# Norm chains between layers and at the end cut into halves, their squares moved forward, and one split of the last down projection made early

## The chip, the cores and the metric

The kernel runs on one core of a Trainium2 chip, in float32 throughout. The metric is the device time of one execution in microseconds; the times shown are medians of several runs. TensorE's clock has two levels here, 1.2 and 2.4 GHz; the profile gives what was granted as a share of the upper one.

## The reference

Two transformer blocks stand one behind the other, for 512 tokens of width 1024 (batch 1). What matters here is how they begin and end:

```python
def _rmsnorm(x, g):
    y = x * rsqrt(mean(x * x, axis=-1) + 1e-6)
    return y * g

# first block
h  = _rmsnorm(x, g_pre_mix)
...                                            # retention, spatial gating, merged
x  = x + _rmsnorm(merged @ w_out, g_post_mix)  # 1024 x 1024
h2 = _rmsnorm(x, g_pre_ffn)
x  = x + _rmsnorm(mlp(h2) @ w_down, g_post_ffn)  # 2816 x 1024, mlp starts with h2 @ w_up
# second block
h  = _rmsnorm(x, attn_norm_w)
...                                            # two kinds of attention, mixed
x  = x + mix @ w_out                           # 1024 x 1024, no norm behind it
h2 = _rmsnorm(x, mlp_norm_w)
u  = relu(h2 @ w_up)                           # 1024 x 4096
x  = x + (u * u) @ w_down                      # 4096 x 1024
return _rmsnorm(x, final_norm_w)
```

## The kernel before

**Products.** Each float32 operand of a large product is split into a high and a low part of the matmul's reduced float32 (`split`, line 145: ScalarE copies the high part, VectorE subtracts to get the low part), and a product is three matmuls: high high, high low, low high (lines 243 to 247). Weights come in units of 128 x 1024 values (512 KB) through three raw buffers; each is split as well, first part on ScalarE (line 220), second part on VectorE or, for some, on GpSimd (line 208). `W.advance` emits the second parts of units whose first parts are there and then further first parts, up to three units ahead of the one in use.

**Two kinds of stages.** `dense_a` gives features on the partitions and all 512 tokens as columns, 24 matmuls of 512 columns for a group of 128 features; with `first=4` the first four groups are done for tokens 0 to 255 before tokens 256 to 511. `dense_bs` gives tokens on the partitions; at the second block's start it takes token tiles (0, 1) ahead of (2, 3), in 12 matmuls of 256 columns per weight unit and tile. `down` (line 341) gives tokens on the partitions and 1024 columns in eight PSUM banks, two halves c = 0, 1 for each of four token tiles t. It runs over K outermost, but the last four K tiles go by token: for each (t, c) twelve matmuls, then a tick, then `finish(t, c)`. So the tiles' results come one after the other, each half 2.7 us apart.

**The order of work.** All instructions are emitted in the order in which the program is written, and each engine takes its own in that order. Side work is written as generators (class `Weave`): a task yields how long it waits, in units of a group of 24 matmuls, and `tick(w)` counts this down for all tasks; one whose count reaches zero emits its next piece at that point. `tick` of the kernel first calls `W.advance`. A tick is thus no time but a place in the queues.

**The chains between layers.** Behind `w_out` and `w_down` of the first block, `finish` runs `post_chain`: `post_norm` (line 485) takes the Square of the first PSUM half with its sum over the row (ScalarE), and when the second half is done the Square of that; GpSimd adds the two sums (line 492), scales and adds EPS (line 440) and takes the power -1/2 (line 441); VectorE multiplies each half by it and by g (`y`, line 497); the sum x + y is done by GpSimd for the first half and by VectorE for the second (line 499). After a wait of 0.5 follows `norm_T` (line 450) for the next layer: Square of the whole row of 1024 (line 447), the two GpSimd operations, after 0.5 `xn` in one VectorE instruction (line 454), after 0.5 eight transposes on TensorE (line 460) into two PSUM banks and the split of each bank (lines 147, 148). `dense_a` and `dense_bs` finish the chains of the tiles that they need first. Behind `w_out_2` there is no norm ahead of the sum: `finish` adds PSUM to x (line 1209) and starts `norm_T`. At the start `norm_T` takes the tiles of x as they land.

**The last down projection.** Its left operand, the 32 feature tiles of `u2`, is split in pairs by `lazy` (line 827): `pair(kp)` makes pair kp, where it isn't there, and kp + 1, in a buffer of the pool `big`. The first call, at the stage's beginning, makes pairs 0 and 1. `finish` (line 1234) adds PSUM to x, takes the Square of the half, and after the second half GpSimd forms the factor; VectorE multiplies both halves by it and by g (line 1250), and each half goes out by a DMA of its own (256 KB), the first issued by SyncE, the second by ScalarE (line 1251).

Of the kernel before, what the change touches and what calls it, by code (L numbers as in the profile page):

```python
# [8 lines left out]
F32R = mybir.dt.float32r  # L9
# [51 lines left out]
class Weave:  # L61
    """Side work emitted between groups of dense matmuls. A task yields how long to wait, in units
    of a group of 24 matmuls of 512 columns."""
# [44 lines left out]
def tile_kernel(  # L108
# [36 lines left out]
    def split(hi, lo, src, eng=None):  # L145
        """src = hi + lo exactly, both rounded to the matmul's reduced float32."""
# [40 lines left out]
    class Stream:  # L187
# [24 lines left out]
        def advance(self, lead):  # L212
            """second parts of the units whose first parts are there, then the next first parts"""
# [29 lines left out]
    def mm(q, lhs, rhs, start, stop):  # L243
        """float32 product of split operands: hi hi + hi lo + lo hi."""
# [4 lines left out]
    class Act:  # L249
        """split activations, features on partitions: [P, K, T] as halves of four tiles of K."""  # L250
# [12 lines left out]
    def dense_a(units, act, evac, first=0, K=KD, pend=None):  # L263
        """features x tokens; of the first so many features, half of the tokens before the rest."""
# [45 lines left out]
    def dense_bs(chunks, act, groups, pend=None):  # L310
        """tokens x columns, K outermost; all chunks for one group of token tiles after the other"""
# [29 lines left out]
    def down(src, K, act_pair, finish):  # L341
        """tokens x 1024 columns: K outermost but for the last four tiles, which go by tokens."""
# [36 lines left out]
    def gload(name, eng=None):  # L379
        """g on every partition."""  # L380
# [53 lines left out]
    def rpow(src, scale, name):  # L434
        """1 / sqrt(scale src + EPS)"""
        r = sm(1, name)
        if scale == 1.0:
            nc.gpsimd.tensor_scalar(r, src, EPS, None, op0=ALU.add)
        else:
            nc.gpsimd.tensor_scalar(r, src, scale, EPS, op0=ALU.mult, op1=ALU.add)  # L440
# [3 lines left out]
    def rms(xt):  # L444
        """1 / rms of the rows"""
        ss = sm(1, "ss")
        nc.scalar.activation(junk, xt, AF.Square, accum_out=ss)
# [851 lines left out]
```

## Time and profile before

| | |
|---|---|
| three runs | 1616.9 us median (1616.67 to 1617.52) |
| span of the profiled execution | 1614.6 us (its own time isn't given apart; the median of the runs is 2.3 us longer than this span) |
| granted TensorE clock, mean | 0.993 |
| TensorE busy | 1577.2 us, 7832 matmuls |
| VectorE, ScalarE, GpSimd busy | 762.3, 614.3, 330.6 us |

The page's other parts show that the transfers take a third of the DMA engines' time or less after the start. A row of a timeline gives start, duration, engine, source line, operation, the tile written and those read with their shapes, the number of instructions merged (x2), and in brackets how long the engine was idle before and for what it waited. PE is TensorE, DVE VectorE, ACT ScalarE, POOL GpSimd; a q behind the name is its queue of DMA issues.

### The profile page before, as it was taken

Reading aid. Unit: us, or ns where it says so; the run is one execution under the profiler, and the core shown is the slowest. Engines: PE = TensorE matmul, PEld = TensorE weight load, DVE = VectorE, ACT = ScalarE, POOL = GpSimd, SP = SyncE. Lnnn points to the kernel's source line nnn. Section 1 sums busy time; section 2 is a strip of 40 time slices with the busy share of each in tenths; the row PEclk is TensorE's granted clock in tenths of the full one; section 3 lists DMA queues with packets and bytes.
Section 4 is the critical chain, followed back from the end, with each engine's and each line's share of the span. In section 5 each row is a group of like instructions: output and inputs, shape, how many; then the busy total and the mean of one; then the engine's idle time right before and its main releaser. Section 6 shows DMA issues by size and latency. Waiting matters only on the chain.

```text
span 1614.6 us, 19745 instructions
## 1 busy us (share of the span) xinstructions
PE 1577.2 (98%) x7832; PEld 1320.6 (82%) x7832; DVE 762.3 (47%) x1305; ACT 614.3 (38%) x1012; POOL 330.6 (20%) x301
## 2 busy tenths in 40 slices
PE   8999999999999999999999999999999999999998
PEld 7888888888887888888887887777877988878886
DVE  4247322453546454555335788768443322233333
ACT  4233223322324433333334366675833322233322
POOL 1015000241004111211004443333244210010000
PEclk9999999999999999999999999999999999999999
DMA  7322332213442233334321412222133333332221
GB/s 210 104 92 65 92 118 85 73 53 91 127 147 65 79 92 102 94 92 136 117 95 56 144 53 53 79 59 74 65 126 95 92 104 97 86 118 96 100 92 52
DMA packets 187323, 152.27 MB, mean 94 GB/s; under 512 B 5232, under 2 KB 157424, under 8 KB 186720
## 3 DMA queue, kind: packets, MB, share of 16 engines
q1 hardware_dynamic: 184784, 143.65, 29.4%
q0 software_dynamic: 1584, 5.70, 1.0%
q10 hardware_dynamic: 864, 1.67, 0.3%
q8 instruction: 61, 1.00, 0.3%
q14 instruction: 30, 0.25, 0.1%
HBM read 146.81 MB, written 4.19 MB: 94 GB/s over the span
## 4 chain that ended last, share of the span: by engine, by line
PE 83%; DVE 8%; ACT 3%; POOL 2%; issue 2%; DMA 1%; SPq 0%; DVEq 0%; POOLq 0%; ACTq 0%
PE ps L245 26%; PE ps L246 26%; PE ps L247 25%; DMA wr<-in_w_in_dram 1%; PE ps L973 1%; PE ps L1064 1%; DVE work L990 1%; PE ps L1055 1%; PE ps L466 1%; PE ps L733 1%; POOL Ya L1188 1%; ACT pr L1034 1%; ACT wh L220 1%; POOL rstd L441 1%; DVE xs L499 1%
## 5 line engine op out<-in xcount | busy, mean ns | idle before, releaser
L220 ACT ACTIVATE wh<-wr 128x1024 fp32r<-128x1024 f32 (+1 forms) x259 | 271.0, 1051 | 250.0 <-PE ps L247 130.9
L208 DVE TENSOR_TENSOR wl<-wr,wh 128x1024 fp32r<-128x1024 f32 (+1 forms) x212 | 257.8, 1226 | 178.9 <-ACT wh L220 178.8
L245 PE MATMUL ps<-wh,ls 128*128 128x512 f32 x432 | 168.4, 390 | 1.2 <-ACT ls L147 1.2
L247 PE MATMUL ps<-wh,ls 128*128 128x512 f32 x432 | 168.2, 389 | 0.3 <-DVE ls L148 0.3
L246 PE MATMUL ps<-wl,ls 128*128 128x512 f32 x432 | 168.1, 389 | 0.0
L246 PE MATMUL ps<-h2Tl,wh 128*128 128x512 f32 (+1 forms) x384 | 142.7, 372 | 0.3 <-DVE h2Tl L148 0.3
L245 PE MATMUL ps<-h2Th,wh 128*128 128x512 f32 (+1 forms) x384 | 142.8, 372 | 0.0
L247 PE MATMUL ps<-h2Th,wl 128*128 128x512 f32 (+1 forms) x384 | 142.6, 371 | 0.0
L208 POOL TENSOR_TENSOR wl<-wr,wh 128x1024 fp32r<-128x1024 f32 x47 | 114.8, 2449 | 134.6 <-ACT wh L220 134.4
L245 PE MATMUL ps<-hTh,wh 128*128 128x512 f32 (+1 forms) x288 | 107.3, 373 | 0.2 <-ACT hTh L147 0.2
L246 PE MATMUL ps<-hTl,wh 128*128 128x512 f32 (+1 forms) x288 | 105.7, 367 | 0.5 <-DVE hTl L148 0.3
L247 PE MATMUL ps<-hTh,wl 128*128 128x512 f32 (+1 forms) x288 | 105.5, 366 | 0.0
L245 PE MATMUL ps<-h3Th,wh 128*128 128x512 f32 (+1 forms) x288 | 105.4, 366 | 0.0
L246 PE MATMUL ps<-h3Tl,wh 128*128 128x512 f32 (+1 forms) x288 | 105.3, 365 | 0.0
L247 PE MATMUL ps<-h3Th,wl 128*128 128x512 f32 (+1 forms) x288 | 105.2, 365 | 0.0
L245 PEld LDWEIGHTS ps<-wh,ls 128*128 128x128 f32 x432 | 81.1, 188 | 18.4 <-ACT ls L147 1.6
L247 PEld LDWEIGHTS ps<-wh,ls 128*128 128x128 f32 x432 | 81.1, 188 | 17.7 <-DVE ls L148 0.8
L246 PEld LDWEIGHTS ps<-wl,ls 128*128 128x128 f32 x432 | 81.1, 188 | 16.6
L857 ACT ACTIVATE hid<-ps,cols 128x512 f32<-128x512 f32 x44 | 34.3, 781 | 144.8 <-PE ps L247 144.8
L858 DVE SCALAR_TENSOR_TENSOR hid<-ps,cols,hid 128x511 f32<-128x511 f32 x44 | 33.0, 749 | 116.8 <-ACT hid L857 116.8
L865 POOL TENSOR_TENSOR act<-hid 128x512 f32<-128x512 f32 x22 | 45.2, 2055 | 194.1 <-DVE hid L860 180.1
L246 PEld LDWEIGHTS ps<-h2Tl,wh 128*128 128x128 f32 x384 | 72.3, 188 | 13.0 <-DVE h2Tl L148 0.6
(293 smaller groups left out, 3253.7 us busy)
## 6 DMA issues: line engine op xcount, KB each, us to landing
wr<-in_w_in_dram SPq DMA_DIRECT2D x86, 512.0 KB, 3.7
wr<-in_w_up_dram SPq DMA_DIRECT2D x76, 512.0 KB, 4.0
wr<-in_w_down_dram SPq DMA_DIRECT2D x54, 512.0 KB, 3.6
wr<-in_w_out_dram SPq DMA_DIRECT2D x16, 512.0 KB, 3.6
wr<-in_w_sgu_o_dram SPq DMA_DIRECT2D x8, 512.0 KB, 4.1
wr<-in_w_ret_o_dram SPq DMA_DIRECT2D x8, 512.0 KB, 4.0
g<-in_rows_dram POOLq DMA_DIRECT2D x6, 512.0 KB, 6.9
x<-in_x_dram SPq DMA_DIRECT2D x4, 512.0 KB, 8.3
```

What stands on the lines that cost most here:

```text
L208: eng.tensor_tensor(lo, self.raw.pop(i), hi.bitcast(F32), ALU.subtract)
L220: nc.scalar.activation(hi, self.raw[self.n_hi], AF.Copy)
L245: nc.tensor.matmul(q, lhs[0], rhs[0], start=start, stop=False)
L246: nc.tensor.matmul(q, lhs[0], rhs[1], start=False, stop=False)
L247: nc.tensor.matmul(q, lhs[1], rhs[0], start=False, stop=stop)
L441: nc.gpsimd.tensor_tensor(r, r, nhalf, ALU.pow)
L466: nc.tensor.transpose(q[:, i * P:(i + 1) * P], src[:, i * P:(i + 1) * P], ident)
L499: eng.tensor_tensor(xrow(t)[:, sl], xrow(t)[:, sl], y[:, sl], ALU.add)
L733: nc.tensor.matmul(o, kz[:, d, c - d, :], vc[c], start=True, stop=True)
L857: nc.scalar.activation(o, q, AF.Identity, bias=col("conv_b", f), scale=col("conv_w1", f))
L858: nc.vector.scalar_tensor_tensor(o[:, 1:], q[:, :T - 1], col("conv_w0", f), o[:, 1:], ALU.mult, ALU.add)
L865: nc.gpsimd.tensor_tensor(act[fa // 4][:, fa % 4, :], a, b, ALU.mult)
```

## The change

The mean is taken inside the Square: ScalarE scales by 1/sqrt(1024) before it squares, so that the accumulated sum is the mean's share of a half, and one GpSimd instruction adds the two halves and EPS (`rpow2`). Every Square and `xn` goes by halves of 512. In `post_norm` both sums x + y are VectorE's, and the Square of each x half is emitted right behind it; its results are handed on to `norm_T`, which then begins with the factor. `norm_T` by itself emits its Squares first and the factor a quarter of a group later; before, the factor's operations were emitted together with the Square. `down` ticks twice for each (t, c), 0.25 in the middle of the twelve matmuls and 0.25 at the end. Pair 0 of the last down projection is split behind the Relu of feature tile 28, in two buffers of the temporary pool `tp`. In the last `finish` the tile t = 3 gets its first half multiplied by g when c = 0 is done, and ScalarE scales this by the factor while VectorE does the second half; the first half now goes out by ScalarE's queue, the second by SyncE's.

```diff
-                tick(0.5)
+                    if kp == n - 2:          # inside the loop over the tail's K pairs
+                        tick(0.25)
...
+                tick(0.25)
                 wv.cur = 0
                 finish(t, c, q2[t])
...
+    def rpow2(ss, name):
+        r = sm(1, name)
+        nc.gpsimd.tensor_scalar(r, ss[:, 1:2], ss[:, 0:1], EPS, op0=ALU.add, op1=ALU.add)
+        nc.gpsimd.tensor_tensor(r, r, nhalf, ALU.pow)
+        return r
+
+    def square(src, acc):
+        w = src.shape[-1]
+        nc.scalar.activation(junk[:, :w], src, AF.Square, scale=D ** -0.5, accum_out=acc)
...
-    def norm_T(t, xt, g, dst, lag=0.5):
-        r = rms(xt)
-        yield lag
+    def norm_T(t, xt, g, dst, lag=0.5, ss=None):
+        if ss is None:
+            ss = sm(2, "ss")
+            for c in range(2):
+                square(xt[:, c * 512:(c + 1) * 512], ss[:, c:c + 1])
+            yield 0.25
+        r = rpow2(ss, "rstd")
         xn = tmp([P, D], "xn")
-        nc.vector.scalar_tensor_tensor(xn, xt, r, g, ALU.mult, ALU.mult)
+        for c in range(2):
+            sl = slice(c * 512, (c + 1) * 512)
+            nc.vector.scalar_tensor_tensor(xn[:, sl], xt[:, sl], r, g[:, sl], ALU.mult, ALU.mult)
         yield lag
...
     def post_norm(t, q, g):
         ss = sm(2, "ss2")
-        nc.scalar.activation(junk[:, :512], q[0], AF.Square, accum_out=ss[:, 0:1])
+        square(q[0], ss[:, 0:1])
         yield 99
-        nc.scalar.activation(junk[:, :512], q[1], AF.Square, accum_out=ss[:, 1:2])
-        s1 = sm(1, "ss1")
-        nc.gpsimd.tensor_tensor(s1, ss[:, 0:1], ss[:, 1:2], ALU.add)
-        r = rpow(s1, 1.0 / D, "rstd2")
+        square(q[1], ss[:, 1:2])
+        r = rpow2(ss, "rstd2")
         y = tmp([P, D], "y")
+        sx = sm(2, "ss")
         for c in range(2):
             sl = slice(c * 512, (c + 1) * 512)
             nc.vector.scalar_tensor_tensor(y[:, sl], q[c], r, g[:, sl], ALU.mult, ALU.mult)
-            eng = (nc.gpsimd, nc.vector)[c]
-            eng.tensor_tensor(xrow(t)[:, sl], xrow(t)[:, sl], y[:, sl], ALU.add)
-        yield 0.5
+            nc.vector.tensor_tensor(xrow(t)[:, sl], xrow(t)[:, sl], y[:, sl], ALU.add)
+            square(xrow(t)[:, sl], sx[:, c:c + 1])
+        yield 0.75
+        return sx
...
-                yield from post_norm(t, q, g)
-                yield from norm_T(t, xrow(t), g_next, dst)
+                sx = yield from post_norm(t, q, g)
+                yield from norm_T(t, xrow(t), g_next, dst, ss=sx)
...
+        def make_small(kp):
+            h_, l_ = (tmp([P, 2, T], "ls", F32R) for _ in range(2))
+            for k in range(2):
+                split(h_[:, k, :], l_[:, k, :], get(2 * kp + k))
+            made[kp] = lambda k, a, b: (h_[:, k, a:b], l_[:, k, a:b])
...
         (nc.vector if f % 2 else nc.gpsimd).tensor_tensor(u2at(f), s, s, ALU.mult)
+        if f == 28:
+            lz2.make_small(0)
...
         if c == 0:
-            ssq[t] = sm(2, "ss2")
-        ss = ssq[t]
+            ssq[t] = sm(2, "ss2"), tmp([P, D], "o")
+        ss, o = ssq[t]
+        last = t == NT - 1
         nc.vector.tensor_tensor(xt, xt, q2[c], ALU.add)
-        nc.scalar.activation(junk[:, :512], xt, AF.Square, accum_out=ss[:, c:c + 1])
+        square(xt, ss[:, c:c + 1])
         if c == 0:
+            if last:
+                nc.vector.tensor_tensor(o[:, sl], xt, g_fin[:, sl], ALU.mult)
             return
...
-            nc.vector.scalar_tensor_tensor(o[:, sl], xrow(t)[:, sl], r, g_fin[:, sl], ALU.mult, ALU.mult)
-            (nc.sync, nc.scalar)[c].dma_start(out=out[t * P:(t + 1) * P, sl], in_=o[:, sl])
+            if last and h == 0:
+                nc.scalar.activation(o[:, sl], o[:, sl], AF.Copy, scale=r)
+            else:
+                nc.vector.scalar_tensor_tensor(o[:, sl], xrow(t)[:, sl], r, g_fin[:, sl], ALU.mult, ALU.mult)
+            (nc.scalar, nc.sync)[h].dma_start(out=out[t * P:(t + 1) * P, sl], in_=o[:, sl])
```

## Rows read from the trace of the kernel before

**Rows 1.** The page's line of busy times: engine, us (share of span), instructions.
```profile
PE 1577.2 (98%) x7832; PEld 1320.6 (82%) x7832; DVE 762.3 (47%) x1305; ACT 614.3 (38%) x1012; POOL 330.6 (20%) x301
```
**Rows 2.** TensorE's waits, whole span: who waited for whom, us, times, longest.
```profile
PE ps L460 <- DVE xn L454: 12.2, 11, 3.2
...
PE ps L245 <- ACT ls L147: 1.2, 1, 1.2
```
**Rows 3.** Timeline of TensorE at boundary 1, 483 to 530 us.
```profile
504.06 1.09 PE L460 MATMUL ps<-ident,xn 128*128 128x128 f32 x8 [0.63 <-DVE xn L454]
...
513.02 1.06 PE L460 MATMUL ps<-ident,xn 128*128 128x128 f32 x8 [1.68 <-DVE xn L454]
...
520.74 1.06 PE L460 MATMUL ps<-ident,xn 128*128 128x128 f32 x8 [0.91 <-DVE xn L454]
```
**Rows 4.** Timeline of ScalarE at boundary 1.
```profile
488.64 0.60 ACT L490 ACTIVATE junk<-ps 128x512 bf16<-128x512 f32 x1 [2.09 <-PE ps L247]
...
493.39 1.06 ACT L447 ACTIVATE junk<-xs 128x1024 bf16<-128x1024 f32 x1 [4.07 <-DVE xs L499]
...
497.53 1.09 ACT L147 ACTIVATE h2Th<-ps 128x512 fp32r<-128x512 f32 x2 [1.54 <-PE ps L460]
500.62 1.06 ACT L447 ACTIVATE junk<-xs 128x1024 bf16<-128x1024 f32 x1 [2.01 <-DVE xs L499]
...
510.34 1.05 ACT L220 ACTIVATE wh<-wr 128x1024 fp32r<-128x1024 f32 x1
```
**Rows 5.** Timeline of VectorE at boundary 1.
```profile
490.56 1.41 DVE L497 SCALAR_TENSOR_TENSOR y<-ps,rstd,g 128x512 f32<-128x512 f32 x2 [5.10 <-POOL rstd L441]
492.00 1.22 DVE L499 TENSOR_TENSOR xs<-xs,y 128x512 f32<-128x512 f32 x1
...
507.60 1.27 DVE L148 TENSOR_TENSOR h2Tl<-ps,h2Th 128x512 fp32r<-128x512 f32 x2
...
517.38 1.21 DVE L208 TENSOR_TENSOR wl<-wr,wh 128x1024 fp32r<-128x1024 f32 x1
519.31 1.28 DVE L454 SCALAR_TENSOR_TENSOR xn<-xs,rstd,g 128x1024 f32<-128x1024 f32 x1 [0.72 <-POOL rstd L441]
```
**Rows 6.** Timeline of GpSimd at boundary 1.
```profile
491.39 1.29 POOL L499 TENSOR_TENSOR xs<-xs,y 128x512 f32<-128x512 f32 x1 [0.86 <-DVE y L497]
...
510.15 1.41 POOL L441 TENSOR_TENSOR rstd<-rstd,nhalf 128x1 f32<-128x1 f32 x1
```
**Rows 7.** Boundary 2: timelines; then stretches: PE, PEld, DVE, ACT, POOL, PEclk, DMA.
```profile
857.28 0.60 ACT L490 ACTIVATE junk<-ps 128x512 bf16<-128x512 f32 x1 [2.09 <-PE ps L247]
...
881.41 1.09 PE L460 MATMUL ps<-ident,xn 128*128 128x128 f32 x8 [2.10 <-DVE xn L454]
...
891.51 1.09 PE L460 MATMUL ps<-ident,xn 128*128 128x128 f32 x8 [0.19 <-DVE xn L454]
...
882.00:887.00 5.00, 5.00 (x32) 5.00 (x30) 3.83 (x5) 2.88 (x5) 3.83 (x9) 0.66 0.34 121
...
480.00:530.00 50.00, 46.34 (x284) 40.70 (x283) 27.90 (x32) 20.93 (x39) 16.35 (x24) 1.00 0.22 64
```
**Rows 8.** Timeline of TensorE where the last down projection begins.
```profile
1430.34 0.39 PE L246 MATMUL ps<-h3Tl,wh 128*128 128x512 f32 x1
1430.57 0.39 PE L247 MATMUL ps<-h3Th,wl 128*128 128x512 f32 x1
...
1433.21 0.50 PE L247 MATMUL ps<-wh,ls 128*128 128x512 f32 x1 [0.31 <-DVE ls L148]
```
**Rows 9.** Behind the last matmul: timelines; then one stretch, columns as in rows 7.
```profile
1608.74 0.19 POOL L1245 TENSOR_TENSOR ss<-ss 128x1 f32<-128x1 f32 x1 [4.33 <-ACT junk L1241]
...
1609.87 1.41 DVE L1250 SCALAR_TENSOR_TENSOR o<-xs,rstd,g 128x512 f32<-128x512 f32 x2 [2.03 <-POOL rstd L441]
1610.65 0.33 SPq L1251 DMA_DIRECT2D out_dram<-o  x1
...
1611.50:1612.00 0.50, 0.00 (x0) 0.00 (x0) 0.00 (x0) 0.00 (x0) 0.00 (x0) 0.50 0.96 360
```

More of the change, by code (lines that the diff above doesn't have):

```diff
@@ L432, in tile_kernel, with rpow @@
     nc.gpsimd.dma_start(out=rb[:, 1, :], in_=rows("b_spatial"))
-    def rpow(src, scale, name):
+    def rpow(src, name):
         r = sm(1, name)
[L437 to L440, printed above, removed]
+        nc.gpsimd.tensor_scalar(r, src, EPS, None, op0=ALU.add)
         nc.gpsimd.tensor_tensor(r, r, nhalf, ALU.pow)
         return r
-    def rms(xt):
-        ss = sm(1, "ss")
-        nc.scalar.activation(junk, xt, AF.Square, accum_out=ss)
-        return rpow(ss, 1.0 / D, "rstd")
-    def norm_T(t, xt, g, dst, lag=0.5):
-        r = rms(xt)
-        yield lag
+    def rpow2(ss, name):
[13 more added lines that the diff above has]
+        r = rpow2(ss, "rstd")
         xn = tmp([P, D], "xn")
-        nc.vector.scalar_tensor_tensor(xn, xt, r, g, ALU.mult, ALU.mult)
+        for c in range(2):
+            sl = slice(c * 512, (c + 1) * 512)
+            nc.vector.scalar_tensor_tensor(xn[:, sl], xt[:, sl], r, g[:, sl], ALU.mult, ALU.mult)
         yield lag
@@ L539, in z_norm @@
         nc.vector.bn_aggr(mv, st.rearrange("p (a b) -> p a b", a=2))
-        r = rpow(mv[:, 1:2], 1.0, "rz")
+        r = rpow(mv[:, 1:2], "rz")
         yield 0.5
@@ L759, in retention @@
                 mvs.append(mv)
-                rs.append(rpow(mv[:, 1:2], 1.0, "rr"))
+                rs.append(rpow(mv[:, 1:2], "rr"))
         yield 1
@@ L841, in pair @@
             return made[kp]
-        pair.make = make
+        pair.make, pair.make_small = make, make_small
         return pair
@@ L948, in ikw @@
         nc.vector.bn_aggr(mv, st[:, None, :])
-        r = rpow(mv[:, 1:2], 1.0, "rr")
+        r = rpow(mv[:, 1:2], "rr")
         kk = tmp2([P, 5, 64], "ik")
@@ L1228, in relu2 @@
         (nc.vector if f % 2 else nc.gpsimd).tensor_tensor(u2at(f), s, s, ALU.mult)
+        if f == 28:
+            lz2.make_small(0)
+    lz2 = lazy(u2at, 16)
     dense_a(a_units(w_up_2, 0, 32), h3T, relu2, first=4, pend=norms)
@@ L1237, in fin @@
         if c == 0:
-            ssq[t] = sm(2, "ss2")
-        ss = ssq[t]
+            ssq[t] = sm(2, "ss2"), tmp([P, D], "o")
+        ss, o = ssq[t]
+        last = t == NT - 1
         nc.vector.tensor_tensor(xt, xt, q2[c], ALU.add)
-        nc.scalar.activation(junk[:, :512], xt, AF.Square, accum_out=ss[:, c:c + 1])
+        square(xt, ss[:, c:c + 1])
         if c == 0:
+            if last:
+                nc.vector.tensor_tensor(o[:, sl], xt, g_fin[:, sl], ALU.mult)
             return
-        s1 = sm(1, "ss1")
-        nc.gpsimd.tensor_tensor(s1, ss[:, 0:1], ss[:, 1:2], ALU.add)
-        r = rpow(s1, 1.0 / D, "rstd")
-        o = tmp([P, D], "o")
-        for c in range(2):
-            sl = slice(c * 512, (c + 1) * 512)
-            nc.vector.scalar_tensor_tensor(o[:, sl], xrow(t)[:, sl], r, g_fin[:, sl], ALU.mult, ALU.mult)
-            (nc.sync, nc.scalar)[c].dma_start(out=out[t * P:(t + 1) * P, sl], in_=o[:, sl])
-    down(w_down_2, 32, lazy(u2at, 16), fin)
+        r = rpow2(ss, "rstd")
+        for h in range(2):
+            sl = slice(h * 512, (h + 1) * 512)
+            if last and h == 0:
[3 more added lines that the diff above has]
+            (nc.scalar, nc.sync)[h].dma_start(out=out[t * P:(t + 1) * P, sl], in_=o[:, sl])
+    down(w_down_2, 32, lz2, fin)
 _WEIGHTS = ["w_in", "w_ret_o", "w_sgu_o", "w_out", "w_up", "w_down",
```

## The prediction, made before any run of the changed kernel

> **What bounds the kernel now.** First the busy times of the engines: TensorE is at work for 98% of the span [rows 1], so the time is the sum of its matmuls plus its waits, and only what changes a wait, or the tail behind the last matmul, can count. Second the list of TensorE's waits [rows 2]: transposes of a normed tile (line 460) waited for `xn` (line 454) 12.2 us in all. By stretch of the trace 5.7 of it lie at the start (the longest, 3.2, is for x and its norm), 3.2 at the boundary from `w_out` to `w_up` (boundary 1), 2.9 at that from `w_down` to the second block (boundary 2), 0.4 at that from `w_out_2` to `w_up_2` (boundary 3). Another 1.2 us stand ahead of the last down projection, for ScalarE's first split of `u2`. Third the timelines of the four engines at boundary 1 [rows 3 to 6], where the reader is to see which chain each transpose waits for, and in which order the queues were filled.
>
> At boundary 1 a tile's chain runs: Square of the second PSUM half (the first of [rows 4]), three small GpSimd operations, y by halves (1.41 for both [rows 5]), x by halves (one on GpSimd, 1.29, one on VectorE, 1.22, since they slow each other; alone a sum of this kind takes about as long as half of the 1.27 that two subtractions take) [rows 5, 6], Square of the row (1.06 and its accumulator read of 0.19) [rows 4], GpSimd, `xn` (1.28) [rows 5], transposes. TensorE's 24 matmuls of a tile take 5.4 us (0.227 apart, [rows 8]) and its transposes 0.9, while the chain's cycle is 7.2 (from one Square of a row to the next, 493.39 to 500.62 [rows 4]), so four waits appear: 0.63, 0.32, 1.68, 0.91 ([rows 3] has the first, third and fourth). Counted from one issue slot to the next they are 4.4 us with the pipeline's restarts.
>
> **The change part by part.** *Work in a chain.* The sum on GpSimd goes (0.19 and a gap of 0.09: 0.28). The x half moves from GpSimd to VectorE: y, x, y, x in a row, each x after its y, is 0.73 + 0.04 + 0.64 twice, 2.8 us, where y, y, x took 1.41 + 0.03 + 1.22 = 2.7 [rows 5]; so it costs 0.1 and takes 1.29 off GpSimd. The Square by halves lets the first run beside y of the second; behind x only about 0.6, as for the Square of a PSUM half, and the read remain [rows 4] in place of 1.25, a gain of about 0.5. `xn` by halves ends 0.1 later and lets half of the transposes start 0.6 earlier. In a chain by itself this is 1.2 to 1.7 us less.
>
> *Order of the queues.* The squares of x are now emitted at once with y and x of the same tile; before, they came one tick later. And `down` ticks twice per half tile, so with waits of 0.75 and 0.5 the chain's `xn` comes in the middle of the next tile's second half, and the transposes with their splits in the middle of the first half of the tile after that. Those splits (two ScalarE copies, 1.09, and two subtractions, 1.27 [rows 4, 5]) are thus emitted after the *following* tile's y, x and squares. ScalarE works in order: h2T's first parts of tile t-1, which ran as soon as the first four transposes were done (497.53 [rows 4]), now stand behind tile t's second square of x, which waits for VectorE. VectorE works in order too: `xn` of tile t stands behind the second parts of tile t-1, which wait for those copies. Likewise the Square of the next tile's PSUM half stands behind the copies. A cycle is then: two PSUM squares 1.4, GpSimd 0.9 (stretched by up to 0.9 where its small operation meets VectorE: one took 1.41 [rows 6]), y and x 2.8, square 0.7, two copies 1.1: 7.0 to 7.5. It isn't shorter than the 7.2 before.
>
> I laid the four queues out in the new order with these durations, beginning at 488.5. The transposes of tiles 0 and 1 come half a group of matmuls earlier, at 495.4 and 502.6; TensorE waits 0.3 and 0.8 with the halves' second wait. The first matmul of `w_up` waits 0.9 for tile 1's split. Tile 2 is there at 512.6 (before 513.0), after 1.2 us of waiting. Tile 3 loses: its x is done at 516.5 (before 516.3), its second square at 517.2; then ScalarE does a first weight part (1.05 [rows 4]), which before ran while it was idle, then the copies of tile 2 until 519.3; VectorE does tile 2's second parts until 520.1, the weight part (1.21 [rows 5]) until 521.2, `xn`'s first half until 521.9. The transposes start at 521.95 against 520.74 now, and TensorE, which had its matmuls done by 519.5, waits 2.5 and then 0.2 for the second half. All waits come to 5.9 against 4.4: **+1.4 us** (+0.8 to +2.2 by the shortest and longest durations of such operations in the rows).
>
> *Clock.* At boundary 2 a wait of 2.10 was followed by a stretch in which the granted clock fell to the 1.2 GHz level; the five microseconds around it had a mean of 0.66 [rows 7], so 5 x 0.34 = 1.7 us of full speed were lost. At boundary 1 the wait of 1.68 was followed by none: the mean of the 50 us there is 1.00. The new wait of 2.5 lies beyond 2.10; there I add **+1.7 us** (0 to 1.7). The Trainium skill (TensorE: Matmul & The Clock Gate, Why this matters for your kernels) warns only of idle gaps longer than this one; by it the 1.7 would go and the sum would be 1618.0, but the row of 2.10 in this trace differs from it.
>
> *Boundary 2.* The down part is the same. Behind it a column group is 12 matmuls of 256 columns; tile 2's transposes move from behind 24 of them to behind 12, since the first half tick already releases them, while `xn` of tile 2 is ready when it was: the wait of 2.10 grows by the 1.4 that these 12 take. Tile 3's `xn` moves ahead of the second rope, but on GpSimd its small operations now stand behind the first rope's sum, and on VectorE behind tile 2's second parts as at boundary 1: 522.3 in boundary 1's terms, where it was 522.9 (891.51 less 368.64, by which the same Square of a tile, 857.28 and 488.64, stands later [rows 4, 7]). TensorE has 9 matmuls fewer behind it by then (1.35), and the next weight part on VectorE comes after `xn` and the second rope, a further wait of 1.4. All waits there come to 7.9. Before they are 3.9 with their restarts (0.60, 2.10, 0.19 for transposes, 0.3 for a weight part) and 1.5 of slow clock; in the new order the slow stretch lies under VectorE's chain, inside the 7.9: **+2.5 us** (+1.0 to +4.0, as rope and GpSimd operations vary most).
>
> *Boundary 3* has no post norm: the first square needs only its own half, which is there early, and no split stands ahead of the sum. The chain shrinks from 4.2 to about 3.3 us for the first half of the transposes, which come 1.4 earlier: its waits of 0.4 go, **-0.3** (0 to -0.5). *Start:* the squares cost 0.2 more behind x's landing, the transposes start with a half `xn`, 0.6 earlier; VectorE, which also does the second parts, then limits: **-0.1** (-0.4 to +0.3).
>
> *First split of the last down projection.* Two copies and two subtractions move from behind the last Relu to behind that of feature 28. There ScalarE has one Relu and one weight part (1.05) in the 5.4 us of a feature, and the weight parts have three units of lead; the copies pass one first part of weights, which comes 1.1 us later and isn't needed for a group. They take two of three buffers of the temporary pool, free since boundary 3. Its third matmul now starts at 1433.21; at the spacing of 0.23 it could have been 1430.57 + 3 x 0.23 = 1431.26 [rows 8]. **-2.0 us** (0 if a bank or a weight part is late instead, as nothing else is seen to wait there).
>
> *End.* The sum on GpSimd goes, 0.28 [rows 9]. The last tile's first half is multiplied by g early and then only scaled by ScalarE (about 0.6) beside VectorE's second half (0.75), where two took 1.41: its last transfer could start 0.9 earlier. But the first one, now from ScalarE's queue, starts at 1609.6 + 0.6 + 0.1 = 1610.3 against 1610.65, and from 1611.5 the DMA engines are 0.96 busy until both have gone through [rows 9]: the end follows the first start, **-0.35** (to -0.9 if they aren't the limit). The Trainium skill (DMA: Bandwidth & Descriptors, Issuing engines are not separate DMA queues) says so as well: two queues share the engines; by it the sum stays, without it 0.55 us less.
>
> **Sum:** +1.4 + 1.7 + 2.5 - 0.3 - 0.1 - 2.0 - 0.35 = +2.85 us. The profiled span is 1614.6; its own time isn't given apart, and the median of three runs, 1616.9, is 2.3 more for what lies around a span. With 2.3 unchanged: 1617.4 + 2.3 = **1619.7**.
>
> **The rivals.** *The clock holds* (as boundary 1's 1.68 did): 1618.0. For it: 2.5 is my estimate, and part of it is two waits. *The chains win* (faster): the splits' place in ScalarE's queue doesn't hurt, since the squares are done by then; the chain gets its 1.2 to 1.7 per tile. Then half of the 4.4 and of the 3.9 go, with the other gains: -2.2 - 1.95 - 2.0 - 0.75 = -6.9, or 1610.0. For it speaks that each operation by itself is shorter; against it that the copies are emitted behind a square that ends 5.2 us after a tile's last matmul, while the transposes are due 1.4 after it. *Clearly slower:* at boundary 2 the wait of 3.4 for tile 2 and that of 1.6 for tile 3 both end late, and a second stretch at 1.2 GHz falls where TensorE, not VectorE, is the limit: +1.7, 1621.4; it decides once tile 3's transposes there start later than 522.9 in the terms above. *The early split doesn't help*, since the last feature's PSUM bank or a GpSimd weight part is waited for instead: +2.0, 1621.7.
>
> **How the numbers follow.** Forecast 0.40, with 1.5 either way; clock holds 0.20; chains win 0.20; clearly slower 0.14; early split without effect 0.06. A measurement of this kernel can tell 0.2%, 3.2 us: slower means above 1620.1, faster below 1613.7. Slower: 0.36 of the forecast, nearly all of the last two: 0.33. Faster: nearly all of "chains win": 0.19. Same: 0.48. For 8 in 10 the range goes from 1612.8, six tenths of the way from the unchanged time to "chains win", to 1622.4, 1 us above "clearly slower"; the forecast's own range is 1618.2 to 1621.2.
>
> **What would show it.** The first parts of h2T for tile 0 start some 4.5 us after its transposes; line 460's longest wait at boundary 1 is tile 3's, above 2 us, and a granted clock of 0.5 follows; at boundary 2 tile 2's transposes wait over 3 us; the wait of 1.2 ahead of the last down projection is gone; the last two transfers run together. The forecast is wrong if the sum of line 460's waits falls.

## The result, and where the time went

The changed kernel takes 1629.5 us (median of 5 runs, 1628.48 to 1629.81) against 1616.9 (median of 5, 1615.72 to 1617.52): ratio 1.0076, 95% interval 1.0065 to 1.0087. It is slower, as forecast, but by 12.6 us and not by 2.8; 1629.5 lies outside the range (1612.8 to 1622.4). The profiled execution has a span of 1627.7 us, its own time 1629.5, a mean granted clock of 0.986.

Both kernels run the same 6672 matmuls of split products in the same order. So the same matmul's start can be set against itself in the two traces: where the difference stays, nothing was won or lost. It changes in six stretches only, each named in a row here, and is constant to 0.03 us in between; inside the rest of block 2 it rises to 11.5 and falls back (starts in us, before and after):

| matmul | before | after | difference | stage that ends here | its share | predicted |
|---|---|---|---|---|---|---|
| 120 | 33.83 | 36.54 | 2.71 | start | +2.71 | -0.1 |
| 2200 | 535.08 | 541.47 | 6.39 | boundary 1 | +3.68 | +3.1 (1.4 waits, 1.7 clock) |
| 3900 | 913.27 | 923.25 | 9.99 | boundary 2 | +3.60 | +2.5 |
| 4980 | 1237.20 | 1246.87 | 9.67 | rest of block 2 | -0.31 | 0 |
| 5160 | 1269.80 | 1285.01 | 15.20 | boundary 3 | +5.53 | -0.3 |
| 6000 | 1454.64 | 1467.75 | 13.11 | last down projection begins | -2.09 | -2.0 |
| end of span | 1614.60 | 1627.72 | 13.12 | end | +0.01 | -0.35 |

The start and boundary 3 make up 8.6 of the 10.3 us between forecast and trace. The profile after, in the order of the rows before. Busy times and TensorE's waits (rows 1, 2 before): TensorE is busy 7.7 us longer with the same 7832 instructions, at a mean granted clock of 0.986 in place of 0.993; its waits for `xn` rose from 12.2 to 19.0, and that for `ls` is gone.

```profile
PE 1584.9 (97%) x7832; PEld 1327.3 (82%) x7832; DVE 772.7 (47%) x1329; ACT 618.4 (38%) x1045; POOL 316.9 (19%) x281
...
PE ps L471 <- DVE xn L465: 19.0, 13, 3.3
```

Boundary 1 on TensorE, ScalarE and VectorE (answers to [rows 3 to 5]), then two stretches (columns as in [rows 7]). Tile 0's split starts at 503.34, 4.65 us behind its transposes (498.69), since it stands behind tile 1's squares (the second at 502.71); tile 3's `xn` (524.59) stands behind tile 2's second parts and a weight part, and its transposes wait 2.36. A stretch at the 1.2 GHz level follows (mean 0.66 in the 5 us).

```profile
498.69 1.32 PE L471 MATMUL ps<-ident,xn 128*128 128x128 f32 x8 [0.64 <-DVE xn L465]
505.96 1.32 PE L471 MATMUL ps<-ident,xn 128*128 128x128 f32 x8 [0.45 <-DVE xn L465]
516.14 1.23 PE L471 MATMUL ps<-ident,xn 128*128 128x128 f32 x8 [0.84 <-DVE xn L465]
525.48 1.23 PE L471 MATMUL ps<-ident,xn 128*128 128x128 f32 x8 [2.36 <-DVE xn L465]
...
502.71 0.63 ACT L453 ACTIVATE junk<-xs 128x512 bf16<-128x512 f32 x1 [0.67 <-DVE xs L508]
...
503.34 1.06 ACT L147 ACTIVATE h2Th<-ps 128x512 fp32r<-128x512 f32 x2
...
522.25 1.29 DVE L148 TENSOR_TENSOR h2Tl<-ps,h2Th 128x512 fp32r<-128x512 f32 x2 [2.28 <-ACT h2Th L147]
523.46 1.22 DVE L208 TENSOR_TENSOR wl<-wr,wh 128x1024 fp32r<-128x1024 f32 x1
524.59 1.41 DVE L465 SCALAR_TENSOR_TENSOR xn<-xs,rstd,g 128x512 f32<-128x512 f32 x2
...
522.00:526.00 4.00, 1.64 (x14) 1.33 (x12) 3.75 (x6) 1.65 (x3) 0.00 (x0) 1.00 0.03 5
526.00:531.00 5.00, 5.00 (x30) 4.95 (x30) 2.33 (x3) 1.19 (x2) 0.00 (x0) 0.66 0.72 209
```

Boundary 2 (answers to [rows 7]): tile 2's transposes wait 3.27, where it was 2.10.

```profile
888.40 1.72 PE L471 MATMUL ps<-ident,xn 128*128 128x128 f32 x8 [3.27 <-DVE xn L465]
898.64 1.32 PE L471 MATMUL ps<-ident,xn 128*128 128x128 f32 x8 [0.61 <-DVE xn L465]
901.13 0.42 PE L246 MATMUL ps<-wl,hT2h 128*128 128x328 f32 x1 [1.01 <-DVE wl L208]
```

Boundary 3, first before (VectorE, GpSimd, ScalarE), which no row ahead of the prediction shows: `xn` of tile 2 begins 0.08 us ahead of two weight parts (second parts of weight units) on GpSimd. GpSimd has its factor done at 1251.95 and then still waits for ScalarE's first part of the unit.

```profile
1251.99 1.29 DVE L454 SCALAR_TENSOR_TENSOR xn<-xs,rstd,g 128x1024 f32<-128x1024 f32 x1 [2.18 <-POOL rstd L441]
1253.19 0.68 DVE L1209 TENSOR_TENSOR xs<-xs,ps 128x512 f32<-128x512 f32 x1
...
1251.40 0.55 POOL L441 TENSOR_TENSOR rstd<-rstd,nhalf 128x1 f32<-128x1 f32 x1
1252.07 5.82 POOL L208 TENSOR_TENSOR wl<-wr,wh 128x1024 fp32r<-128x1024 f32 x2
...
1250.95 1.99 ACT L220 ACTIVATE wh<-wr 128x1024 fp32r<-128x1024 f32 x2
```

The same after (VectorE, GpSimd, ScalarE, TensorE, a stretch). GpSimd begins 0.04 us *ahead* of `xn`, whose two halves now take 5.65 us in place of 1.41. TensorE waits 1.59 and 2.03 for them, and some 7 us at the 1.2 GHz level follow.

```profile
1259.61 5.65 DVE L465 SCALAR_TENSOR_TENSOR xn<-xs,rstd,g 128x512 f32<-128x512 f32 x2 [1.89 <-POOL rstd L447]
...
1259.02 0.56 POOL L447 TENSOR_TENSOR rstd<-rstd,nhalf 128x1 f32<-128x1 f32 x1
1259.57 5.14 POOL L208 TENSOR_TENSOR wl<-wr,wh 128x1024 fp32r<-128x1024 f32 x2
...
1258.44 1.05 ACT L220 ACTIVATE wh<-wr 128x1024 fp32r<-128x1024 f32 x1
...
1262.65 0.63 PE L471 MATMUL ps<-ident,xn 128*128 128x128 f32 x4 [1.59 <-DVE xn L465]
1265.31 1.11 PE L471 MATMUL ps<-ident,xn 128*128 128x128 f32 x4 [2.03 <-DVE xn L465]
...
1264.00:1271.00 7.00, 5.69 (x21) 5.11 (x22) 3.84 (x5) 2.40 (x6) 1.01 (x2) 0.51 0.47 136
```

The start. Before (VectorE, GpSimd), `xn` of tile 1 was well ahead of GpSimd's weight part:

```profile
10.91 1.28 DVE L454 SCALAR_TENSOR_TENSOR xn<-x,rstd,g 128x1024 f32<-128x1024 f32 x1 [2.99 <-POOL rstd L441]
...
11.79 2.63 POOL L208 TENSOR_TENSOR wl<-wr,wh 128x1024 fp32r<-128x1024 f32 x1 [0.91 <-ACT wh L220]
```

After (VectorE, GpSimd, TensorE), the part gets in between the halves of tile 1: the first half runs at 11.53, GpSimd's weight part begins at 11.81, the second half waits for its end (3.51 us for both, TensorE waits 2.53 and 1.65).

```profile
11.53 3.51 DVE L465 SCALAR_TENSOR_TENSOR xn<-x,rstd,g 128x512 f32<-128x512 f32 x2 [3.02 <-POOL rstd L447]
...
11.81 2.67 POOL L208 TENSOR_TENSOR wl<-wr,wh 128x1024 fp32r<-128x1024 f32 x1 [0.32 <-ACT wh L220]
...
12.33 1.11 PE L471 MATMUL ps<-ident,xn 128*128 128x128 f32 x4 [2.53 <-DVE xn L465]
15.09 1.11 PE L471 MATMUL ps<-ident,xn 128*128 128x128 f32 x4 [1.65 <-DVE xn L465]
```

The last down projection (answers to [rows 8]) begins without a wait, and the last two transfers (answers to [rows 9]) start together.

```profile
1445.77 0.39 PE L247 MATMUL ps<-h3Th,wl 128*128 128x512 f32 x1
1445.99 0.39 PE L245 MATMUL ps<-wh,ls 128*128 128x512 f32 x1
...
1621.87 0.30 POOL L446 TENSOR_SCALAR rstd<-ss 128x1 f32<-128x1 f32 x1 [4.50 <-ACT junk L453]
...
1622.85 0.72 ACT L1273 ACTIVATE o<-o,rstd 128x512 f32<-128x512 f32 x1 [1.07 <-POOL rstd L447]
1622.85 0.75 DVE L1275 SCALAR_TENSOR_TENSOR o<-xs,rstd,g 128x512 f32<-128x512 f32 x1 [1.89 <-POOL rstd L447]
1623.60 0.37 ACTq L1276 DMA_DIRECT2D out_dram<-o  x1
1623.63 0.33 SPq L1276 DMA_DIRECT2D out_dram<-o  x1
```

### The profile page after: what moved, and what is told of

Same layout as the page of the kernel before. It is cut to its first block, busy times and chain, and to the rows that moved or that the text cites. A ratio compares the mean times of both kernels' runs of the same rounds, so it can differ in the third digit from the quotient of the medians.

```text
span 1627.7 us, 19791 instructions
## 1 busy us (share of the span) xinstructions
PE 1584.9 (97%) x7832; PEld 1327.3 (82%) x7832; DVE 772.7 (47%) x1329; ACT 618.4 (38%) x1045; POOL 316.9 (19%) x281
## 4 chain that ended last, share of the span: by engine, by line
PE 54%; DVE 7%; ACT 3%; POOL 2%; issue 1%; POOLq 0%; ACTq 0%; DVEq 0%
PE ps L246 17%; PE ps L245 17%; PE ps L247 17%; PE ps L991 1%; PE ps L1082 1%; DVE work L1008 1%; PE ps L1073 1%; POOL Ya L1206 1%; ACT wh L220 1%; ACT pr L1052 1%; DVE sums L1060 0%; ACT junk L453 0%; DVE y L507 0%; DVE xn L465 0%; DVE xs L508 0%
## 5 line engine op out<-in xcount | busy, mean ns | idle before, releaser
L446 POOL TENSOR_SCALAR rstd<-ss 128x1 f32<-128x1 f32 x28 | 11.5, 410 | 387.0 <-ACT junk L453 386.9
L245 PEld LDWEIGHTS ps<-h2Th,wh 128*128 128x128 f32 x384 | 73.1, 190 | 13.1 <-ACT h2Th L147 0.6
```

The source lines that it names most:

```text
L245: nc.tensor.matmul(q, lhs[0], rhs[0], start=start, stop=False)
```

## The experiments

Eleven more kernels were run. Their shares by stage, as in the first table, each against the trace of the kernel before; medians, and ratios to that kernel's runs on the same chip (its medians there 1616.9 to 1618.3).

| run | start | b. 1 | b. 2 | rest | b. 3 | last down | median us | ratio, 95% interval |
|---|---|---|---|---|---|---|---|---|
| changed kernel | 2.71 | 3.68 | 3.60 | -0.31 | 5.53 | -2.09 | 1629.5 | 1.0076 (1.0065, 1.0087) |
| whole_xn | 1.14 | 3.69 | 3.33 | -0.27 | 3.06 | -2.09 | 1624.9 | 1.0040 (1.0025, 1.0054) |
| vector_parts | 3.03 | 2.19 | 3.57 | 1.09 | -0.79 | -2.09 | 1622.8 | 1.0034 (1.0021, 1.0048) |
| old_norms | -1.11 | 2.19 | 3.61 | -0.49 | 0.00 | -2.09 | 1621.0 | 1.0022 (1.0013, 1.0032) |
| squares_later | 2.58 | -1.27 | 0.55 | 0.71 | 5.63 | -2.09 | 1621.6 | 1.0029 (1.0018, 1.0040) |
| whole_square | -0.67 | 3.69 | 3.29 | -0.45 | 4.93 | -2.09 | 1625.8 | 1.0052 (1.0035, 1.0069) |
| order_only | -0.20 | 5.94 | 5.61 | 0.86 | 0.01 | 0.01 | 1628.5 | 1.0066 (1.0053, 1.0080) |
| start_fill | 1.93 | 3.71 | 3.61 | -0.54 | 5.33 | -2.09 | 1627.8 | 1.0063 (1.0047, 1.0078) |
| mended | -0.77 | -1.56 | -0.04 | -0.15 | -0.79 | -2.09 | 1611.6 | 0.9967 (0.9955, 0.9980) |
| mended_fill | -0.12 | -1.55 | -0.02 | 0.07 | -0.81 | -2.09 | 1611.9 | 0.9964 (0.9952, 0.9977) |
| mended_b2_36 | 0.44 | -1.53 | 4.08 | 0.19 | -0.80 | -2.09 | 1616.3 | 0.9992 (0.9983, 1.0001) |
| mended_b2_48 | 0.78 | -1.53 | 1.30 | -0.09 | -0.80 | -2.09 | 1614.6 | 0.9983 (0.9974, 0.9992) |

Two theories are tried, each at its own places. A (start, boundary 3): `xn` is held up by GpSimd's weight parts. D (boundaries 1 and 2): the order of ScalarE's queue, as predicted. Rivals: the quarter ticks (B), the halves themselves (C), the length of the chain whatever its order (E), the changed operations (F), TensorE's clock (G) and, against G, VectorE's chain whatever the clock (H).

The start alone scatters: six kernels in it have the code of before (the kernel before itself, old_norms, order_only, mended and the last two) and lie between -1.1 and +0.8. At the first product it scatters less: these six begin it at 13.87 to 14.46, the changed kernel at 15.86. The rest of block 2, which the edits hardly touch, lies between -0.5 and +1.1. The other columns repeat to 0.3 where the code is the same, but for 3.68 and 2.19 at boundary 1 and 0.55 (squares_later) and -0.04 (mended) at boundary 2, of which below.

**whole_xn: `xn` in one instruction at the start and at boundary 3.**

```diff
+        parts = 1 if ss is None else 2
...
-        for c in range(2):
-            sl = slice(c * 512, (c + 1) * 512)
+        for c in range(parts):
+            sl = slice(c * D // parts, (c + 1) * D // parts)
```

> Changed kernel with xn in one instruction again at the start and at boundary 3 (halves kept at boundaries 1 and 2). Theory A, VectorE's xn is held up by a GpSimd weight part that gets in first or between its halves: at the start xn of tile 1 begins at 11.5, ahead of GpSimd's part at 11.8, and takes about 1.3 instead of 0.75 and 2.84; -1.5 to -2.5 us there. At boundary 3 xn of tile 2 begins 0.04 after the first of two GpSimd parts, so it still waits for that one (2.9 in place of 1.3), but no longer for the second: -2.0 to -3.5 us. Total 1623.5 to 1626.0. Rival B, the order of the queues after `down`'s quarter ticks is what costs there, with the lower clock behind it: no change at either place, 1628.5 to 1630.5.

The total lies in theory A's range, boundary 3 too (-2.5), the start at its lower end (-1.6). At boundary 3 (VectorE, GpSimd of this run) GpSimd again came first, by 0.03, and `xn` waited for one part, not for two; the second part then waited for `xn`.

```profile
1258.05 3.43 DVE L466 SCALAR_TENSOR_TENSOR xn<-xs,rstd,g 128x1024 f32<-128x1024 f32 x1 [1.89 <-POOL rstd L447]
...
1258.02 5.70 POOL L208 TENSOR_TENSOR wl<-wr,wh 128x1024 fp32r<-128x1024 f32 x2
```

**vector_parts: these weight parts off GpSimd.**

```diff
-ON_POOL = (0, 228, 229)
+ON_POOL = (228, 229)
...
-                eng = nc.gpsimd if i in ON_POOL else self.eng
+                eng = nc.gpsimd if i in ON_POOL else nc.vector if i in (195, 196) else self.eng
```

> Changed kernel, with the second parts of weight units 0, 195 and 196 (those that GpSimd does at the start and at boundary 3) on VectorE; xn stays in halves. Theory A: each half of xn takes 0.75 everywhere, tile 2's wait at boundary 3 goes; start -1.5 to -2.5, boundary 3 -4 to -6, less up to 1.2 for each part that VectorE does ahead of an xn: 1621.5 to 1625.0. Rival B (queue order and clock): VectorE gets 3.7 us more work, nothing is regained: 1629 to 1632. Rival C, the halves themselves cost it (longer squares, two instructions): as B.

The total lies in theory A's range. Boundary 3: all of it came back, and 0.79 more, beyond the range. The units were named one too low: the two parts that meet `xn` are units 196 and 197. Unit 196 went to VectorE, behind `xn`; 197 stayed on GpSimd and, with no part ahead of it, began only when its first part was there (1261.14). `xn`'s halves at 1259.83 take 1.42 again. At the start theory A failed: `xn` was free and the first product began at 14.05 as before, but TensorE then waited 1.41 for unit 0's second part, now late on VectorE, and ran at the 1.2 GHz level until 22.8: +3.03. So this run doesn't show what the part's hold of `xn` costs there.

```profile
1259.83 1.42 DVE L465 SCALAR_TENSOR_TENSOR xn<-xs,rstd,g 128x512 f32<-128x512 f32 x2 [1.89 <-POOL rstd L447]
...
16.76 0.58 PE L247 MATMUL ps<-hTh,wl 128*128 128x256 f32 x1 [1.41 <-DVE wl L208]
```

**old_norms: the norm at the start and at boundary 3 as before.**

```diff
         if ss is None:
-            ss = sm(2, "ss") ...       # squares by halves, rpow2, xn by halves
+            ss = sm(1, "ss") ...       # Square of the row, two constants, xn in one
```

> Changed kernel with the norm at the start and at boundary 3 written as before (one Square of the row, mean by GpSimd's two constants, one xn); boundaries 1 and 2, `down`'s quarter ticks, the early split and the end stay. Theory A: start and boundary 3 come back to the kernel before, so 1629.5 - 2.5 - 6.0 = 1621.0, with 1619.5 to 1623.0. What is left over 1616.9 is then boundaries 1 and 2 (+7.5), less the early split (-2.3) and what block 2 gives back. Rival B (quarter ticks and queue order cost it at boundary 3 too): start comes back alone, 1626 to 1628.

1621.0, as theory A has it; boundary 3 is 0.00 with `down`'s quarter ticks still there, so rival B is out there. (The trace is of a run of 1618.5, 2.5 below the median; which stage the other runs lose that in isn't shown.)

**whole_square: one Square and one constant at the start and at boundary 3, `xn` still in halves.**

```diff
         if ss is None:
-            ss = sm(2, "ss")
-            for c in range(2):
-                square(xt[:, c * 512:(c + 1) * 512], ss[:, c:c + 1])
-            yield 0.25
-        r = rpow2(ss, "rstd")
+            ss = sm(1, "ss")
+            square(xt, ss)
+            r = rpow(ss, "rstd")
+            yield lag
+        else:
+            r = rpow2(ss, "rstd")
```

> Changed kernel, at the start and at boundary 3 with one Square of the row and GpSimd's add of one constant, as before, but xn still in halves. Theory A in its sharper form: at boundary 3 the two engines' order hangs on GpSimd's add (0.30 with two operands, 0.19 with constants), since in the kernel before GpSimd then waits 0.12 for the weight unit's first part. With 0.19 the first half of xn goes ahead, GpSimd's part begins during it, and only the second half waits, for one part (2.4): boundary 3 +1.5 to +3.0, with tile 2's first four transposes on time. At the start xn of tile 1 begins at 10.9 and its second half at 11.6, ahead of GpSimd's part at 11.8: no hold, start -1.0 to +1.0. Total 1622 to 1625. Rival C, the halves of xn cost nothing and the halves of the squares everything: boundary 3 0, start 0, 1620.5 to 1621.5. Rival: neither matters alone, boundary 3 stays at +5.5.

The start came out as the theory has it: `xn` of tile 1 begins at 10.67, both halves are done before GpSimd's part at 11.66. Boundary 3 (VectorE, GpSimd) did not: 4.93 is the third course named, in which it stays, and the total lies above the range. `xn` begins 0.03 ahead of GpSimd by the trace, and both its halves are held up all the same. GpSimd's add of one constant took 0.22 here and not 0.19, and the power 0.57 and not 0.55; these 0.05 are what the lead lacks of the 0.08 before.

```profile
1257.55 5.71 DVE L466 SCALAR_TENSOR_TENSOR xn<-xs,rstd,g 128x512 f32<-128x512 f32 x2 [2.23 <-POOL rstd L440]
...
1256.64 0.22 POOL L439 TENSOR_SCALAR rstd<-ss 128x1 f32<-128x1 f32 x1 [5.50 <-ACT junk L453]
...
1257.58 5.13 POOL L208 TENSOR_TENSOR wl<-wr,wh 128x1024 fp32r<-128x1024 f32 x2
```

Over the kernels with two GpSimd parts there, `xn` ahead by 0.08 (before, old_norms) and 0.09 (order_only) goes through in 1.28 or 1.29; ahead by 0.03, or behind by 0.03 to 0.05 (whole_xn, the changed kernel, squares_later), it is held. In these traces the border is thus a lead of between 0.03 and 0.08. Cutting `xn` is not needed for the loss there (3.06 in whole_xn), only makes it larger (5.53).

**squares_later: the squares of x a quarter tick behind x.**

```diff
-            square(xrow(t)[:, sl], sx[:, c:c + 1])
-        yield 0.75
+        yield 0.25
+        for c in range(2):
+            square(xrow(t)[:, c * 512:(c + 1) * 512], sx[:, c:c + 1])
+        yield 0.5
```

> Changed kernel, with the two squares of x emitted a quarter tick after y and x (the wait of 0.75 becomes 0.25 and 0.5), so that tile t's transposes and splits stand ahead of tile t+1's squares on ScalarE. xn comes at the same tick. Theory D, the order of the queues makes the loss at boundaries 1 and 2: tile 3's wait at boundary 1 falls from 2.36 to under 1 us and no half-clock stretch follows; tile 2's wait at boundary 2 falls from 3.27 to 1.5 to 2.5; the two boundaries cost 2 to 4 us instead of 7.5: 1624.0 to 1627.0. Rival E, the chain's work and not its order sets the cycle: no change within 1 us, 1628.5 to 1630.5.

Theory D, and more than it expected: the two boundaries cost -0.7 together in place of +7.3, with the same instructions; only the place of the squares in ScalarE's queue is another. TensorE at boundary 1 of this run, tiles 0 to 3:

```profile
498.56 1.32 PE L471 MATMUL ps<-ident,xn 128*128 128x128 f32 x8 [0.65 <-DVE xn L465]
505.47 1.33 PE L471 MATMUL ps<-ident,xn 128*128 128x128 f32 x8
...
514.38 1.23 PE L471 MATMUL ps<-ident,xn 128*128 128x128 f32 x8 [0.58 <-DVE xn L465]
521.90 1.23 PE L471 MATMUL ps<-ident,xn 128*128 128x128 f32 x8 [0.54 <-DVE xn L465]
```

**order_only: the order alone, put on the kernel before** (with `down`'s two quarter ticks as in the change).

```diff
             eng.tensor_tensor(xrow(t)[:, sl], xrow(t)[:, sl], y[:, sl], ALU.add)
-        yield 0.5
+        r = rms(xrow(t))
+        yield 0.75
+        return r
```

> Kernel before, with the order of the change alone: `down` ticks by quarters in its tail, the whole-row Square of x is emitted at once with x (its GpSimd mean too) and the wait after it is 0.75. Operations as before: half of x on GpSimd, mean by GpSimd's sum, xn in one instruction, late first split of the last down projection, end as before. Theory D, the order alone costs the two boundaries: boundary 1 +2 to +4 us, boundary 2 +3 to +4 us, so 1622 to 1625, with start and last down projection unchanged against the kernel before. Rival F, the halves and x on VectorE cost it: boundaries within 1 us of the kernel before, 1616 to 1618.

The order costs 5.94 and 5.61, beyond theory D's range, and rival F is out. With the operations of the change it costs 3.68 and 3.60: these gain 2.3 and 2.0 of it back (at boundary 2 with 3.4 us less at the lower clock level, so part of the 2.0 can be the clock). It also is the control for the early split: without it the last down projection stays at 0.01.

**start_fill: TensorE kept at work through its waits at the start.**

```diff
-    for _ in range(26):
+    for _ in range(42):
...
+            for _ in range(FILL.get((dst.name, t, half), 0)):   # tile 1: 22 and 12
+                nc.tensor.transpose(q[:, :P], ident, ident)
```

> Changed kernel, with 16 more transposes of the identity before x is there, and 22 and 12 ahead of tile 1's two halves at the start, written where the real ones then go (TensorE works through its waits; the chain is the same, nothing else changes). Theory G, what is left of the start's loss is TensorE's lower clock, since TensorE stands idle before tile 0 and tile 1: the stretch of 13.65 us at the 1.2 GHz level goes or shrinks to 3 to 4 us, and the start costs 0 to +1.2 instead of +2.7: 1627.3 to 1628.5. Rival H, VectorE's chain behind the blocked xn limits the start, whatever the clock: start stays at +2.2 or more, 1629 or slower.

The start lies between the two, the total in theory G's range. The same 8 us at the start, first in this run, then in the changed kernel: the granted clock is 1.00 instead of 0.50, yet the start gained only 0.8, within its scatter.

```profile
8.00:16.00 8.00, 6.73 (x58) 6.05 (x56) 5.36 (x7) 4.47 (x9) 3.53 (x3) 1.00 1.12 339
```
```profile
8.00:16.00 8.00, 3.82 (x17) 3.01 (x17) 4.98 (x5) 4.07 (x8) 3.54 (x3) 0.50 1.11 338
```

**mended: three edits together**, those of squares_later, of old_norms (at the start alone) and of vector_parts (at boundary 3 alone).

```diff
-                eng = nc.gpsimd if i in ON_POOL else self.eng
+                eng = nc.gpsimd if i in ON_POOL else nc.vector if i in (195, 196) else self.eng
...
-    norms = [run(norm_T(t, x0[t // 2][:, t % 2, :], g_pre, hT)) for t in range(2)]
+    norms = [run(norm_T(t, x0[t // 2][:, t % 2, :], g_pre, hT, old=True)) for t in range(2)]
```

> Changed kernel with three edits: squares of x a quarter tick later (as in the run with later squares), norm at the start as before, second parts of units 195 and 196 on VectorE. By the stages of the runs so far: start 0 (-1 to +1), boundary 1 -1.3, boundary 2 +0.6, block 2 -0.5 to +0.7, boundary 3 -0.8, early split -2.1, end 0, so -3.6 against the kernel before: 1613.4, 1612.0 to 1615.0. Rival: the edits aren't independent (a gain at one boundary moves a half-clock stretch into the next), 1615 to 1617.

1611.6, faster than both kernels: 0.9967 (0.9955 to 0.9980), and below the range, as the two boundaries and the start gave more than was put down for them (the start within its scatter). The shares of the table add up to it: -0.77 - 1.56 - 0.04 - 0.15 - 0.79 - 2.09 = -5.4.

**mended_fill: mended, with TensorE's waits at the start and at tile 2 of boundary 2 filled.**

```diff
+FILL = {('hT', 1, 0): 24, ('hT2', 2, 0): 16}      # and 42 transposes at the start, as in start_fill
```

> As the kernel with the three edits, with 16 more transposes of the identity at the very start, 24 ahead of tile 1's at the start and 16 ahead of tile 2's at boundary 2 (in TensorE's wait of 2.0 us there). Theory G: the half-clock stretches at 12 us and behind boundary 2 go: -1.0 to -1.7 us each, 1610.5 to 1612.0. Rival H: the chains limit, not the clock: within 0.5 us of the kernel with the three edits; or the fillers last longer than the wait and delay the real transposes: +1 us.

Rival H. The time at the 1.2 GHz level within the span fell from 22.6 to 11.9 us, and the time didn't move: where it fell, the chains set it. Mended has no such stretch behind boundary 2, so the fillers tell nothing of the clock's price there. But squares_later has the same code there and such a stretch (3.4 us): 0.55 against -0.04, so it costs 0.6 there.

**mended_b2_36, mended_b2_48: tile 2's transposes at boundary 2 later in TensorE's queue.**

```diff
-                yield from norm_T(t, xrow(t), g_next, dst, ss=sx)
+                yield from norm_T(t, xrow(t), g_next, dst, lag=0.75 if late and t == 2 else 0.5, ss=sx)
```

> Kernel with the three edits, and at boundary 2 tile 2's transposes a quarter tick later, so behind 24 instead of 12 matmuls of 256 columns. In the kernel with the three edits they wait 1.98 us. If that wait is time lost because too little work stands ahead (the step of the prediction that made boundary 2 dearer than boundary 1), 12 more matmuls of 0.11 us take 1.4 of it: wait 0.5 to 0.7, boundary 2 -1.0 to -1.5 us, 1610.1 to 1610.6. Rival: VectorE's chain (tile 3's y, x and xn, the ropes, the weight parts) ends boundary 2 whatever TensorE does meanwhile; the wait moves to a later place: within 0.4 us of 1611.6.

> As the run before, half a tick later: tile 2's transposes behind 36 matmuls. If the wait alone counts: none left, boundary 2 -1.6 to -2.0 us, 1609.6 to 1610.0. Rival (VectorE's chain ends the boundary): within 0.4 us of 1611.6, or later by up to 1 us, as tile 2's splits then stand behind tile 3's operations.

The rival, and worse than it said. The wait of tile 2 goes, from 1.98 to 0.45 (mended_b2_36), but tile 2's splits now stand behind tile 3's operations, and tile 3's transposes wait 4.05 where mended has 0.29: boundary 2 is 4.1 dearer, with the later place 1.3 (tile 3 then waits 2.70). Part of both can be the clock: 6.8 and 3.4 us at the lower level there, none in mended.

```profile
878.95 1.32 PE L481 MATMUL ps<-ident,xn 128*128 128x128 f32 x8 [0.45 <-DVE xn L475]
889.88 1.97 PE L481 MATMUL ps<-ident,xn 128*128 128x128 f32 x8 [4.05 <-DVE xn L475]
```

## Why the prediction was wrong

**Boundary 3 (-0.3, measured +5.53): the step that failed.** The prediction counted the chain's operations by themselves ("shrinks from 4.2 to about 3.3") and named no other work of GpSimd there. Before, GpSimd had two weight parts waiting at the same instant as `xn`, and `xn` went first by 0.08 us, since GpSimd's factor was done (1251.95) just before ScalarE's first part of that unit. Afterwards GpSimd's add of two operands takes 0.30 in place of 0.19, the first part is there (1259.49) when the factor is done (1259.58), and GpSimd goes straight on, 0.04 ahead; in whole_square 0.05 of lateness was enough. Whoever comes second waits for the whole of the other's instruction: both halves of `xn` together took 5.65 for 1.41. Shown by the runs: in one piece it waits for one part (+3.06), with the first part off GpSimd for none (-0.79), with the old norm it wins again (0.00). The chain by itself did shrink: with nothing in its way it is worth -0.79, where -0.3 was put down. The Trainium skill has this rule (SBUF — State Buffer, SBUF: two separate sides): a VectorE instruction with two SBUF inputs and a GpSimd instruction that reads SBUF take a shared pair of ports as a lock, which the first to start holds for its whole instruction. The trace agrees, but for the 0.03 of whole_square; the prediction reckoned with the effect only for GpSimd's small operations and for the sum x + y, where it costs tenths.

**Start (-0.1, measured +2.71): the same omission.** "VectorE then limits" left out GpSimd's part of unit 0. The squares by halves, put at 0.2, and GpSimd's longer add delay `xn` of tile 1: from its first Square (8.97) to `xn` (11.53) it is 2.56, where old_norms has 2.10 and whole_square 2.15. Its second half then meets that part. With one Square the loss is gone though `xn` is in halves (-0.67, within the start's scatter); with `xn` in one piece behind two squares it is 1.14. At the first product 1.81 is lost (15.86 against 14.05), beyond the scatter there. How the rest divides, and what of it is the clock (0.8 by start_fill), can't be told from the scatter.

**Boundary 1 (+3.1, measured +3.68): right in mechanism and place.** Every sign that was named is there: the 4.65 us to the split, tile 3's wait of 2.36 (2.5 forecast), the new stretch at the lower level. The two terms can be told apart, since old_norms and vector_parts have the same code there and no such stretch: waits 2.19 (at the upper end of 0.8 to 2.2: from tile 0 on the chain comes 0.6 to 0.8 later than laid out, as 498.69 and 525.48 less the start's 2.71 against 495.4 and 521.95), clock 1.49 (1.7 forecast). Tile 3 waits 2.38 in those two and 2.38 in whole_xn, which has the stretch: whether "the clock holds" comes true hung on more than the length of that wait.

**Boundary 2 (+2.5, measured +3.60): right in sign and cause, short by 1.1.** squares_later takes 3.05 of it away, so the order of ScalarE's queue is the cause there too. Tile 2's wait grew about as forecast (3.27, 3.5 forecast). Tile 3's chain was mis-sized: its transposes start at 898.64, which less the 6.39 lost until then is 892.25; laid out was 522.3 in boundary 1's terms, which is 890.94 here. They are 1.3 later. Whether the 1.4 for "12 instead of 24 matmuls" was a cost by itself stays open: with more work ahead of tile 2 its wait went, but that move also put its splits behind tile 3's operations, and the boundary got dearer. A wait of TensorE inside this boundary can't simply be counted as loss.

**Early split (-2.0, measured -2.09)** was right: the difference stays at 15.20 through the stage in which the copies now lie, so they are hidden there. **End (-0.35, measured +0.01):** GpSimd's add took 0.30, ScalarE's scale 0.72 and not 0.6, so the first transfer starts 0.16 earlier (1623.60 less 13.11, against 1610.65 [rows 9]); the two transfers, now started together, take 2.8 and 2.6 us to land where they took 2.0 and 2.1, and the last landing, 0.05 earlier, isn't seen in the span.

**The rivals.** "Chains win" (0.20) had the operations right and the order wrong: shorter operations gained 2.3 and 2.0 at the boundaries, and with the order mended and the weight parts out of the way the kernel reaches 1611.6. That this is near its 1610.0 is luck in part: boundary 2 gave 0.04 where it had 1.95. "Clearly slower" had tile 3's start at boundary 2 right (523.6 in its terms, beyond its 522.9), but the second stretch at the lower clock didn't come there: 3.4 us in both kernels. None of the rivals had the weight parts of GpSimd, and none of the signs looked at the start or at boundary 3: all of them came, and the sum was 10 us short.

## What to carry to other kernels

Before an operation on a chain is cut in two or moved by tenths, look which instructions of the engine that can hold it up (here GpSimd for VectorE) start within that reach: who goes first can be worth a whole weight part, and a cut lets the other engine in a second time. Where an engine takes its work in order, an instruction emitted early because its own input is nearly ready delays everything emitted behind it; put it behind the work of the previous tile whose result is waited for. And a wait that TensorE shows need not be worth its length: when tile 2's wait at boundary 2 was taken away, the stage got longer.

## What the runs showed of the hardware that was not expected

A VectorE instruction that reads PSUM is not held up by GpSimd: the sum at 1253.19 took 0.68 while GpSimd was in its two parts (5.82), where `xn`, all from SBUF, took 3.43 in place of 1.28 (whole_xn). A lead of 0.03 us by the trace isn't enough to go first, one of 0.08 is. And after the same wait of 2.38 at boundary 1 the granted clock fell to the 1.2 GHz level in one kernel (whole_xn) and held in two others, by one trace each.
